# A planner that leaves room for TensorE's instruction transfers, and the order that comes from it

## The chip, the cores and the metric

The kernel runs on one core of a Trainium2 chip. The metric is the device time of one execution in microseconds (us); the kernel before takes 1061.63 us (median of three runs, 1060.88 to 1062.44). The engines are TensorE (PE in the profile; its weight loads are PEld), VectorE (DVE), ScalarE (ACT), GpSimd (POOL) and SyncE (SP), which issues the transfers of the weights.

## The reference

A trunk of two layers over 256 tokens of width 1024, all in float32. Layer 0 mixes the tokens with an RWKV-7 recurrence, layer 1 with stick-breaking attention; 12 heads of 64 do this, and 4 heads attend to 256 fixed memory tokens.

```python
def swiglu(x, w_gate, w_up, w_down):
    return (jax.nn.silu(x @ w_gate) * (x @ w_up)) @ w_down
...
    for i in range(DEPTH):
        x = layer_norm(ALPHA * x + 0.5 * swiglu(x, ffn1_w_gate[i], ffn1_w_up[i], ffn1_w_down[i]),
                       ln_g[i, 0], ln_b[i, 0])
        ...
        heads = jnp.concatenate([mix, memory_attention(mq, mem_k, mem_v)], axis=-1)
        x = layer_norm(ALPHA * x + heads @ w_out[i], ln_g[i, 1], ln_b[i, 1])
        x = layer_norm(ALPHA * x + 0.5 * swiglu(x, ffn2_w_gate[i], ffn2_w_up[i], ffn2_w_down[i]),
                       ln_g[i, 2], ln_b[i, 2])
```

The recurrence of layer 0, for each head with a 64x64 state (w is a decay, kk a normed key, b = kk * a):

```python
    def step(state, inp):
        r_t, w_t, k_t, v_t, kk_t, b_t = inp
        sa = jnp.einsum('bhij,bhj->bhi', state, kk_t)
        state = (state * w_t[:, :, None, :] - sa[..., :, None] * b_t[..., None, :]
                 + v_t[..., :, None] * k_t[..., None, :])
        return state, jnp.einsum('bhij,bhj->bhi', state, r_t)
```

## The kernel before, in words

**Tiles.** The tokens lie in two halves of 128. The hidden width of a feed-forward part, 2816, is worked in 11 blocks of 256 columns. Most weights are split into a high and a low part in a type that TensorE takes in one pass (float32r), and so are the activations; one 128x128 piece of an activation then meets 512 columns of weights in three products (high by high, low by high, high by low; `mm3`). These are the wide split products, printed as `hi_..`, `lo_..` against `xTh`, `xTl` or another `hi_..`. Products left in plain float32 take two passes and count as two (`raw_..` against `hT_945r`, and the gate, `gup_111r`). Transposes go through TensorE too (`cst` against the tile).

**The mixer of layer 0** (`rwkv`) works on chunks of 64 tokens: it builds a triangular inverse T with small products of 64x64 (12 heads by two chunks give 24 or 48 products in one step), then carries the 64x64 states S along. In the profile's names: `Tt_332r,Lm_333r` is Lm times Tt, whose result Y goes through VectorE or ScalarE into `Y_340r,T_339r` and `T_339r,Y_340r` (T by Y, in both orders); this is done twice, the second time with the larger blocks (`lastl`). `vn_314r,Sk_344r` is Sk by V, `S_113r,qr_377r` the state by queries, `L_345r,Tt_332r` is Tt by X, where X lies in a buffer that the trace calls L. In the text, "Lm.Tt", "T.Y", "S.qr" and "L.Tt" stand for these. Between such steps lie copies and sums on VectorE and ScalarE, each step waiting for the one before. The mixer of one half is issued beside blocks of the feed-forward part of the other half (`alternate`), and the wide products of those blocks fill TensorE while the mixer's steps wait.

**The order.** Nothing is issued when the program is written down. Each instruction is first recorded in a `Plan` as an operation; products that belong together (`together`) form one. `price` gives each its duration on its engine. `order` is a list scheduler: it plays the engines forward with a clock for each, transfers that land one behind the other (`LAND`), a TensorE clock that halves after a window of 3413 ns that was too idle (`WINDOW`), and extra time when TensorE changes between kinds of product. At each step it takes the engine that can go on first and, of the operations that could start there, the one of the least rank:

```python
                t, o = x
                p = o.pri + (t - t_e) * WAIT
```

`o.pri` comes from a table of numbers, `URGENCY`, one for each operation, unpacked in `improve`; the table is the result of a search that was done ahead of time. So the order on every engine, and the buffer that every tile gets, follow from the table and from the times that `order` reckons. `issue` then writes all instructions in that order. As it does so from one line, every instruction has the same line in the profile (L767 before, L787 after), and they are told apart by the names of their tiles.

Of the kernel before, what the change touches and what calls it, by code (L numbers as in the profile page):

```python
# [113 lines left out]
class Op:  # L114
    __slots__ = ("i", "eng", "calls", "took", "lag", "after", "opens", "closes", "pri", "func", "port", "left", "ready",
                 "end", "users", "kb", "turns", "mode", "share", "spent", "fine", "parts", "round", "places", "ways")


class Engine_:
# [11 lines left out]
WINDOW = 3413.0  # L131
ROUNDS = 50
# [3 lines left out]
    'c-l?edDu=>)Iad^B%+Y1P)Q;s6=fbmL?lCo43#-UGDb2Kp(0~4&lJi~B2qFWDnq778YLo%l9KT3-)Fz~dtLAEkLS9Fv(MgZeb;w=*V^Zt`>FG32;'  # L136
    'DOz$(YPZa^&9-K1@rJwg3C~|G)2T%nwPDq@4=kY488JDoO72I{vaGS$!#lSw8>i^Wncjc;RFS<DGLbYwGxd%abIhV<&%4ec$EkBzfF-YySMd&yV@'
    'M>W|dtZaGq)i<eE3Hm5^qa7~hY^Gygl%(wHu5PsSjLeq>%@`%4B=5K%b|GnPl-0=rO$bLnVJj$mf{vI&r4Q#x^_+8Q03nBFLdg|^ZnXxZ~D&~FPy'
    'p^&f$$78y&W5n!$|PwEk3xBq<jo@?{Cb=D92?D^`>#)uedpP=J!S8j>`9XGVhH!1PJMpTeE*p1bN=OL)2(cqb8C_m>6#>4#)i-?6KwBHlD*Dpx+R'
    '3~*j(!S5H{YJBp>}6!rb%_?sWb;=6VON$NV*b`-JPv!=9;ZZ^Q0~ehZ-)zw+IXBu)4<%wHz{KE<}K#&luFmDV0mAW1s?9K!C0lVtPc5OTIjl6qf+'  # L140
    'aBN2i#lE)weMvI^E-`*Jgu*qG<X+zuGXJ^GN%CO9B>CIt*R5S;eF%95C&`{gA!IbZ>=HH^b2WRHR!fp~FNKh+gn3ql@b^t{5%2fl*u4}VHiR&ft('
    'Eg6NkOkWDksU)+fw+nHtxdBNm3u)bIak)<`AZx3*ldLjgLGy9KsP;oq$`lTax5qz8vkFB-eEb;T9OoESV(3jk^MdpRwz&A8`;C2R6dmoa<npOi7Z'
    '=14H-)Kd-KuBoE<M^O+(1$*-&458=h8NwT<QlH^(zLT>ym3e!LLgs>e)3KU9`x$@-6{7G_|c(tx0SIk-as}MSe5a$0A!rfvu@}m%Lo5{ZEAzTZ$o'
    'P4O`c*8OL+MFbHCx)=<l_c4=B7_c;tb<2Oe=!zUbK%_ZoJo=oFLsqrk`go0lDqn3LzpvR!M$lohQ8_Hs%@9T)-t#wo@W{)N!E(|U!Nqimxr(%*D~'
    '?tCpdI1oFu<-dBQVEGS=FgaNtMW-Ebm=+u?JHALWaMFyxxFWHOFyY!pISb7sZk_V_dMSO`7X{rR;?GV0MJx#!yu?!t$XzI%m@C1BH<&)<G0M&fwh'
    'Yj!a_$DgCK#T>uxy@zgy*%{oaAO>y4bU&WFg>z5do+KUK;YYO)t{01U#J6}a`68}oa6POJ;SDj(^(LQ=hA_i=@6v#Q@}o7shv3<Pen~QJaR{eimz'
    '7QBehOg<9Z3_%+ed{^>Q#Il7s4~n&CRD~rITb6j0>I#VH;oH!L2dIt*hwxt`H`Rc{8!T*Vrn?mYW2??df4aWBOs8p13g@*Oz&pzLHK_r`^Nwe>O>'
    'OWBWP24DFaC#quS|8=G)!wXrz!!M*gX3S39RuxAL3%y$wFSJJR2`TJmVIVuls64#q?sInNWkedte^Mp98kw3HLb7%3Lz{f(yjg})T*MzX8I2+|;A'
    'G)>|PUT^A$nhg$))^L)AAt$ono3iC=oP}K7m}o<cyAE1dcUWKi7j9_0ap%&&?4#~JmxP?l4;dx9)A8lJcNsLaP$M(*qh!w0SlZu)Lv}GwAm;012<'
    '04$GNm`u(gi1k~g2xM!epQ$64h>L%!6d599ZT&<RIttqmdJ)1?XG^nQ{orziczaFsC)x%ATW>EX5GG~wE`WL+`ZG#*yV!~}=RiqqacNm64se?AZ4'  # L150
    '>sm>2wjT{(=RfQ};QT-5CdoyypIIYG?%tLjJ{^%HBVc))?WbY2KjLiOqcFTvd^YCB54rlNxQ(xuB>fMCkVU@CS{lNbm+--w-^zswa)06|c0T7kTH'
    '0j*orQHDnp_ut?X7WyKHbnTgpTt4NppSx@4xt)9mh)1q!n^v6MkI{`-L!mPo8w67oW1ZHIDS1>ph-df609L=$G+pKS+{!uq%p3-@KS4P0P>`d0eb'
    'T2$#u+XX$oXnzWgAyhroO!*bSxN%Dn!Z{u||-Y*i5^Yn54)({rfrZMk?@GyLa{mo~3To;$l!{tW2d~Bik$cqW=Z6Hqy%l-1Sw>i!GaGso@d%eByL'
    '1(MT-MWwYtD2Uqm9Gook^PP&`Gn@2_)<R0^<i@GBemimzK+GEx9}n(j&xRcK9&oI<m9(FdS!jQeB9jQljIk@z$ZnlCl<}=N>Kj_@aGx2@E-l_N|X'
    'EKQiJHuIC}QH^Y2x24jEGnPH(YmspG@xO&V_QksH6ziVkplN6qLYPw!TDo4}z*rx4zMH%Y$2)0yg2ad_P$M>dJs65RL%r~VV${`}~R3q7qf(K=1&'
    ';SroTKsT0&*=QKuME7smtIk=wzu2Q^vg}BD7+y&X)u1zK%5SiESdQKDI1b=h<t|CG=%e(I^$U5Y4hG!VCH5m8Ns?d1YQBDE6FXY5_lS7>DG#1x<6'
    'wRr!RO`T*OpHF0*AZIcK{|g(}QkwZo1rjMa}(EZr%##wLb3_lRu4{50laKCI|jpaYb5k_2qgA{mH*@=;Qm@;#gL!{^r*xIOSnaS3KGaqc7>-1{$!'
    '3&J3lQQ|bITylV}IQaDwLO_oXWJ6=RDQ;ilz-D-<de~4uk{8=HVM&Q=ZY;WEpEm=55je~1xc6U_=&Y5SgI@5~%jg83-vwZZVAnmwLyyx-dC;TqRm'
    '!`fe37^99un&75^!grdeSy=5aVgFD2WjIxeCoSK??|sZ!){9vJxli_`GcK3V0tzC?lSgT#~$L}rJ{N+e9z0K^7#H8Tjs?YMT={R$yL@G;oQ}Htj&'
    '(s9D9i^*{u7!&*}8=O*yxc4MqI*H1BA!Xvoi(<oavQt<KKt<X>@fG{dP&I9nS}+u?l&>)#3Q+i`ZQc+F+s+idvwJ@JrBIVY!dW)OdGG}lp>|Kjr*'  # L160
    '@0Ze!oce)@#<ir`!`Rfz`fGe&Tg(o@a=IXOG`0iIY&Z8e?0-G>UgjGKhhcIiBmWP|w@;iK_X-7l*U|Z9jj!$f65oFidsVNcW6ZsF!k=aIw5<2L^='
    'YN#el=LNe9AmDq@>svrFWZr&ScC+J<An%eLxIf;d43I{iXfMgDd^zQgdsyHEy1D^Rs`rdiWWeUbkLmyxw5$1MnN*csn*7cW(WdTXdj;oc&XdzOT-'
    'Gq_+NyS0!-iCiC57-okKgBA3>S$xpC-%zAH`uaG%z&@b-x{>#WEuM4b~h2Fnw{l2i(+9svpb<9}HCQ3qh2yP>2^d5P<$+%<mKR+I{laoW(b2(e~>'
    'e)t5#cRD&V_G@NT#s90HQbh(?@AncpM9r%e$MM9I`Ecx=J@_*7>&UH%I1DU9UCO?Uc{~E#PC6L?8D1F&UpeJT^KbGP8}Q{35S1H;w=0sdjDKkdFc'
    '2q^W~L?+s%_pO+A92^JwptY}Lvo>)7`MziNxc0vdDHy!Ea~@o5?S;{NS6cC|BRCEp)lLnG&16pKfld&c`WY1n>xQba!Ig>N=<jNlvSlk>EqTZ0fX'
    'Tf2pR@M$sV!oCj9ogxROm}iRk+)-bA*zZs%BLCh}yLa=s1MF^|M(=6(P&%{A`d!#j7miu^wv3*Y*Dv&BYkPBM6086C`nGtU<HPs`eAC|ze;fYns^'
    'k0}>R&UxO+8%MH3V0?(-`BYsI!N~^`hFlQydr4<L>zUy1F+9e=A#W8lS$h_TO+RV69R2TkC9UpS^)*J*nS&Tpx5u{F+<OvSFWb0spRtNpZc;?d-c'
    '!E|#Z3E!mi`VX}T<5>Ag%-|DL)4XyE#F<bex6HmLrbsj9bz;nNOnwnz+Os5;u!xVqm`#q!9Opn^Zmbc`789BNXKc?c#!|KwGq3ofNv*LIdY`5<&c'
    '0Lu0aq8KRbiReT_wv0yd*j+4>MJg&jY|aPZh8Gt)HX32gCnJ_^Rw6a=AXf~+A-cZ)K1{Du(OCBvY<W$%pvN|Q!v|Wo*MAj3x})3|0bN-;k6(>{-A'
    'E}V$Yk_Z7Y`xi|GOw&Qdqeu{#rvHdSZx+nd)ke+g^d`k@|2-|!Xv9tF#`wL-|C7Ppl<qv3gv{c0w9`vM#mIX(kd%Uh$8n*Fx^YLnWR<!<|sE%Na('  # L170
    'wZ$Hws&(q~`7Pt;i^r4pkk_->6v-+!{>|^!{)W@-g7|l@n5T=!JqE0!LnYPKcJR2(+-upnN8MagfzRwIgd3A+MZ6Y~f$a@pH6EtrG{-BfJ6$d61='
    'E`&7mUq)S;~(?bZNi$Bk*>#`n>9CdrLk4MO^s<&Kqc6R{YDt&d<fHWv-N#?zjFtxW8%6&*Aw6-!C^$7F^yXzp7gQKCy{9f7ZE;_*zk~_Px0L2=@j'
    '0ya%_WB{Pephwk`N_5r;L40^_EDdzZ2{b;Ax9%=8B8+V%1>oIt8mw4vZFEx@^jo5Jv2KVXhuC0=)eJjN9a+nRcM(^wUa-Sth3;p##JxJ}i7sasy)'
    '+h&?@#@D4@qNIY7o2~PPglx`oA@z|?Xd@5jthJB_s{tJ20tpv^9Rh))10+(+rPqgvG*0>aDlIb;M2{R<NUnrJ~11NBXF8YpElB$>=6_8^%H{|5cn'
    'd^JgrZ>L_gQjr|ZP&^0!lc*b{hC$Xp*9-<_5<euI9giBHq&IY&~pWUe0I5A$ZA7e~Y}BMi>S-?jRd1A5Ahifcvweceq@FjS7=(hIOFqX?ZA<9}dy'
    '8itqSWlz3G?d=5TuYI4L)?_sI2kd%EOoT0YOq_GD`AgqD=Dg>{<x@VbqB-N>6R)>LjYfg+l)pxB`2nuq@~3eQ{IOR&Yrhb$kF|>&=1Whn|Czjjn0'
    'zU}dWier+^Igco_&4QPU<8duBV&NTjLSqhw`<7JzyG)%CL88U)YO%zQ~L6VmnB#^5tEh@1#keIqz0Ev=q;pu9Lg=-5u4hoZ`1ZjJ5OOJR7&s=#Ry'
    '$JwGR~p{1HTO+(&-UR*{KPn++4#{z$6#G3E>`}lZWtYa`6h%=qUEHiAr5aX3_-oeggZ25|<#pve<TzlF+v8OS|#;1pTY~KLie~dXOj{RZrlKyL;{'
    'lpabkNE)~%=4$U8tV%)^ZzfLoCoBmt@RFj?lX1_OlIQBM%>$v+vD)DtYejF%4l)wZjEDXU1<K^ZPJoMFQ$iuxE$2^241s^+hSbYhKsr7^p)bVz}O'
    'F?KE_^weebZNgni{w@2mOy!#Pd(O%B8F_BfyXkm~Plj(cPJnXu*AAANrzJ#^D|A6S_lGSig1<$4)fSrF$s^5IAM(aie{-uKbV&Zc!`*i_%%v<wW&'  # L180
    '@^`6v+|S(EaO{++GqC9bEf`lir5m4#%~$3*&8D^Ty}O?9Z}YWq?4sCDD~PLa$OksvMvs>AZKz)A3%RjhZ}gsc{zbd9&9Db|&O&SSH(vqcZ}HkmZC'
# [106 lines left out]
class Plan:  # L288
# [1604 lines left out]
```

## Time and profile before

| what | value |
|---|---|
| median of three runs | 1061.63 us (1060.88 to 1062.44) |
| profiled execution | 1061.31 us, span 1059.5 us |
| mean granted clock of TensorE | 0.994 |
| busy | TensorE 1041.7 us (98%), VectorE 883.6 (83%), ScalarE 740.9 (70%) |
| products | 6275 |
| instruction transfers of TensorE's queue (q8) | 49, 0.80 MB |
| moved by DMA | 303.19 MB, 286 GB/s on average |

The span is the time from the first to the last instruction in the profile; 1.8 us of the execution lie around it. Times in a row of the timeline are the start and the length of an instruction; the ends of products are modelled and overlap, so that the distance of two starts is what a product costs. A bracket at the end of a row is the idle time of the engine ahead of it, and what ended that.

### The profile page before, as it was taken

What the parts mean: (1) busy time and instruction counts of PE and PEld (TensorE: products, weight loads), DVE (VectorE), ACT (ScalarE), POOL (GpSimd) and SP (SyncE); (2) the same over time, 40 slices, a digit from 0 to 9 for tenths busy, and PEclk for the clock granted to TensorE, in tenths of its full rate; (3) what the DMA queues carried; (4) which work ended last, traced back from release to release, by engine and by line L of the source; (5) the groups of instructions that cost most, each with busy time, mean ns of one, the idle gap of its engine ahead of it and who ended that gap; (6) DMA issues with size and microseconds to landing.
All of it is one profiled execution on the core that took longest, in us unless ns stands there. A gap on an engine that the chain in (4) does not pass through costs nothing.

```text
span 1059.5 us, 17849 instructions
## 1 busy us (share of the span) xinstructions
PE 1041.7 (98%) x6275; PEld 835.5 (79%) x6275; DVE 883.6 (83%) x1241; ACT 740.9 (70%) x1065; POOL 5.3 (0%) x20
## 2 busy tenths in 40 slices
PE   9999999999899999999999999999999999999996
PEld 7888888877688776688888888888778777878885
DVE  6676679999899997898799755469899999976688
ACT  6665559968689887667677544457987998865572
POOL 0000000000000000000000000000000000000000
PEclk9999999999899999999999999999999999999998
DMA  9997869779399788799899966677989989997891
GB/s 327 329 369 242 270 215 352 247 253 336 115 338 328 255 264 290 242 339 329 284 340 366 325 211 215 193 255 254 370 297 313 364 285 304 368 349 258 276 311 67
DMA packets 212684, 303.19 MB, mean 286 GB/s; under 512 B 13892, under 2 KB 159728, under 8 KB 212594
## 3 DMA queue, kind: packets, MB, share of 16 engines
q1 hardware_dynamic: 212050, 301.53, 85.5%
q8 instruction: 49, 0.80, 0.3%
q10 hardware_dynamic: 544, 0.52, 0.2%
q14 instruction: 41, 0.34, 0.1%
HBM read 300.95 MB, written 1.05 MB: 285 GB/s over the span
## 4 chain that ended last, share of the span: by engine, by line
PE 97%; DVE 1%; ACT 1%; DMA 0%; issue 0%; SPq 0%; DVEq 0%; ACTq 0%
PE ps_29r L767 30%; PE ps_30r L767 28%; PE ps_27r L767 8%; PE ps_26r L767 8%; PE ps_3r L767 8%; PE ps_25r L767 8%; PE ps_5r L767 4%; PE ps_6r L767 3%; DMA raw_12r<-in_ffn_w_up_dram 0%; DVE x L767 0%; DVE L_345r L767 0%; SPq L767 0%; ACT hi_10r L767 0%; ACT Lm_333r L767 0%; DVE lo_11r L767 0%
## 5 line engine op out<-in xcount | busy, mean ns | idle before, releaser
L767 PE MATMUL ps_29r<-hi_13r,xTh 128*128 128x512 f32 x64 | 26.3, 411 | 0.0
L767 PE MATMUL ps_29r<-hi_43r,xTh 128*128 128x512 f32 x64 | 26.0, 406 | 0.0
L767 PE MATMUL ps_29r<-lo_14r,xTh 128*128 128x512 f32 x66 | 25.8, 390 | 0.0
L767 ACT ACTIVATE idle_2r<-ps_29r 128x256 f32<-128x256 f32 (+1 forms) x31 | 12.8, 411 | 18.4 <-PE ps_29r L767 18.3
L767 PE MATMUL ps_29r<-hi_46r,xTh 128*128 128x512 f32 x62 | 25.1, 405 | 0.0
L767 PE MATMUL ps_29r<-hi_43r,xTl 128*128 128x512 f32 x64 | 25.1, 392 | 0.0
L767 PE MATMUL ps_29r<-hi_13r,xTl 128*128 128x512 f32 x64 | 25.0, 391 | 0.0
L767 PE MATMUL ps_29r<-hi_46r,xTl 128*128 128x512 f32 x62 | 24.2, 390 | 0.0
L767 PE MATMUL ps_29r<-lo_44r,xTh 128*128 128x512 f32 (+1 forms) x62 | 23.8, 383 | 0.0
L767 PE MATMUL ps_30r<-lo_11r,xTh 128*128 128x512 f32 (+1 forms) x62 | 23.8, 383 | 0.0
L767 PE MATMUL ps_29r<-lo_11r,xTh 128*128 128x512 f32 x58 | 22.8, 392 | 0.7 <-DVE lo_11r L767 0.7
L767 PE MATMUL ps_30r<-hi_46r,xTh 128*128 128x512 f32 (+1 forms) x58 | 23.0, 396 | 0.0
L767 PE MATMUL ps_29r<-hi_7r,xTh 128*128 128x512 f32 x54 | 22.6, 419 | 0.1
L767 PE MATMUL ps_30r<-lo_17r,xTh 128*128 128x512 f32 x58 | 22.6, 390 | 0.0
L767 PE MATMUL ps_29r<-lo_8r,xTh 128*128 128x512 f32 x58 | 22.6, 390 | 0.0
L767 PE MATMUL ps_29r<-lo_17r,xTh 128*128 128x512 f32 x58 | 22.6, 390 | 0.0
L767 PE MATMUL ps_30r<-lo_47r,xTh 128*128 128x512 f32 x58 | 22.6, 390 | 0.0
L767 PE MATMUL ps_30r<-hi_46r,xTl 128*128 128x512 f32 (+1 forms) x58 | 22.2, 383 | 0.0
L767 PE MATMUL ps_30r<-hi_22r,xTh 128*128 128x512 f32 x54 | 22.1, 410 | 0.0
L767 PE MATMUL ps_29r<-hi_16r,xTh 128*128 128x512 f32 x54 | 22.1, 409 | 0.0
L767 PE MATMUL ps_30r<-hi_10r,xTh 128*128 128x512 f32 x54 | 22.1, 409 | 0.0
L767 PE MATMUL ps_29r<-lo_47r,xTh 128*128 128x512 f32 x56 | 21.8, 390 | 0.0
(2125 smaller groups left out, 3922.4 us busy)
## 6 DMA issues: line engine op xcount, KB each, us to landing
raw_21r<-in_ffn_w_down_dram SPq DMA_DIRECT2D x19, 512.0 KB, 5.4
raw_67r<-in_ffn_w_gate_dram SPq DMA_DIRECT2D x32, 256.0 KB, 5.8
raw_67r<-in_ffn_w_up_dram SPq DMA_DIRECT2D x32, 256.0 KB, 6.0
raw_15r<-in_ffn_w_down_dram SPq DMA_DIRECT2D x16, 512.0 KB, 6.0
raw_12r<-in_ffn_w_gate_dram SPq DMA_DIRECT2D x31, 256.0 KB, 4.0
raw_12r<-in_ffn_w_up_dram SPq DMA_DIRECT2D x31, 256.0 KB, 4.6
raw_45r<-in_ffn_w_gate_dram SPq DMA_DIRECT2D x31, 256.0 KB, 6.3
raw_45r<-in_ffn_w_up_dram SPq DMA_DIRECT2D x31, 256.0 KB, 5.5
```

The lines of the kernel that those rows point to most:

```text
L767: fn(*[at(x) for x in a], **{n: at(x) for n, x in k.items()})
```

## The change

The planner gets a model of how TensorE's own instructions arrive. Each operation counts the products that it issues (`count`: one for a transpose or a float32r product, two for a plain float32 one). In `order`, the count of products issued so far runs over edges, at 94.7 and then every 127.1 products. Two edges may not be passed within less than 5500 ns: where they would be, the operation in which the second one lies takes as much longer. Nothing is issued for this; it only changes the clock by which the scheduler chooses. The table of urgencies is another one (298 lines), found with the new clock.

```diff
+FETCH = 5500.0
+CHUNK = 127.1
+CHUNK0 = 94.7
...
 URGENCY = (
-    'c-l?edDu=>)Iad^B%+Y1P)Q;s6=fbmL?lCo43#-UGDb2Kp(0~4&lJi~B2qFWDnq778YLo%l9KT3-)Fz~dtLAEkLS9Fv(MgZeb;w=*V^Zt`>FG32;'
...
+    'c-l?e2iVT#8$R&+Ata(i%E-u!5DjESnUx|+8dhdzLRRskkeN}*%9gC8XegsnW-3L6QWTX{M0xK2=iB=~j{m>ocn|M0zW06I*L9xfbzaZ&eQWe_j6'
...
             o.i, o.eng, o.calls, o.after, o.parts, o.ways = len(self.ops), eng, [], {}, [], {} if either else None
+            o.count = 0
...
             o.mode, o.round = (rows <= 64, m <= 64), st.dtype == F32R
+            o.count += 1 if method == "transpose" or st.dtype == F32R else 2
...
         mode, until, busy, cold = None, WINDOW, 0.0, True
+        issued, edge, crossed = 0, CHUNK0, -FETCH
...
                     until, busy = until + WINDOW, share * rest
+                first, took_, stall = issued, took, 0.0
+                issued += o.count
+                while issued > edge:
+                    at_ = t + stall + took_ * (edge - first) / o.count
+                    if at_ < crossed + FETCH:
+                        stall += crossed + FETCH - at_
+                        at_ = crossed + FETCH
+                    crossed = at_
+                    edge += CHUNK
+                took = took_ + stall
             clock[e] = t + took
```

The operations stay the same; their order, and the buffers, change. TensorE has 6275 products before and after. VectorE gets three instructions more and ScalarE three fewer (copies that may go to either), SyncE issues 873 in both.

On TensorE, in the mixer of layer 0 for the first half, these rows stood between the last T.Y products and the last Lm.Tt products of the inverse (banks are named `ps_..`, x2 is two products in one row):

```order
L767 MATMUL ps_25r<-T_339r,Y_340r 64x64 x2
L767 MATMUL ps_5r<-T_339r,Y_340r 64x64 x2
L767 MATMUL ps_25r<-T_339r,Y_340r 64x64 x2
L767 MATMUL ps_5r<-T_339r,Y_340r 64x64 x2
L767 MATMUL ps_26r<-Tt_332r,Lm_333r 64x64 x2
L767 MATMUL ps_6r<-Tt_332r,Lm_333r 64x64 x2
```

The same place in the new order:

```order
L787 MATMUL ps_26r<-T_339r,Y_340r 64x64 x2
L787 MATMUL ps_5r<-T_339r,Y_340r 64x64 x2
L787 MATMUL ps_30r<-hi_40r,hi_46r 128x512
L787 MATMUL ps_30r<-lo_50r,hi_46r 128x512
L787 MATMUL ps_30r<-hi_40r,lo_47r 128x512
L787 MATMUL ps_30r<-hi_40r,hi_46r 128x512
L787 MATMUL ps_30r<-lo_50r,hi_46r 128x512
L787 MATMUL ps_30r<-hi_40r,lo_47r 128x512
L787 MATMUL ps_25r<-Tt_332r,Lm_333r 64x64 x2
L787 MATMUL ps_6r<-Tt_332r,Lm_333r 64x64 x2
```

Six wide split products of a feed-forward block now stand between the two groups of small ones; the edge after 1493 products lies in the Lm.Tt block in both.

On TensorE, in the mixer of layer 0 for the second half, ahead of the first L.Tt products, before:

```order
L767 MATMUL ps_3r<-vn_314r,Sk_344r 64x64 x2
L767 MATMUL ps_27r<-vn_314r,Sk_344r 64x64 x2
L767 MATMUL ps_3r<-vn_314r,Sk_344r 64x64 x2
L767 MATMUL ps_27r<-vn_314r,Sk_344r 64x64 x2
L767 MATMUL ps_26r<-raw_48r,hT_945r 128x512
L767 MATMUL ps_6r<-L_345r,Tt_332r 64x64
L767 MATMUL ps_5r<-L_345r,Tt_332r 64x64
```

and now:

```order
L787 MATMUL ps_6r<-S_113r,qr_377r 64x64 x2
L787 MATMUL ps_5r<-S_113r,qr_377r 64x64 x2
L787 MATMUL ps_26r<-raw_67r,hT_945r 128x512
L787 MATMUL ps_30r<-hi_7r,xTh 128x512
L787 MATMUL ps_30r<-lo_47r,xTh 128x512
L787 MATMUL ps_30r<-hi_7r,xTl 128x512
L787 MATMUL ps_30r<-hi_7r,xTh 128x512
L787 MATMUL ps_30r<-lo_47r,xTh 128x512
L787 MATMUL ps_30r<-hi_7r,xTl 128x512
L787 MATMUL ps_5r<-L_345r,Tt_332r 64x64
L787 MATMUL ps_6r<-L_345r,Tt_332r 64x64
```

The block of Sk.V products that stood here now comes behind the L.Tt products, and six wide split products stand between S.qr and L.Tt; the edge after 3145 products lies in the L.Tt block in both.

More of the change, by code (lines that the diff above doesn't have):

```diff
@@ L115 @@
     __slots__ = ("i", "eng", "calls", "took", "lag", "after", "opens", "closes", "pri", "func", "port", "left", "ready",
-                 "end", "users", "kb", "turns", "mode", "share", "spent", "fine", "parts", "round", "places", "ways")
+                 "end", "users", "kb", "turns", "mode", "share", "spent", "fine", "parts", "round", "places", "ways", "count")
 class Engine_:
@@ L141 @@
[L141 to L145, printed above, removed]
```

291 lines of the change are left out of this document (150 added, 141 removed).

## The prediction

> **What bounds the kernel now.** I read the page first: the busy times, the slices and the chain that ended last.
>
> ```profile
> span 1059.5 us, 17849 instructions
> PE 1041.7 (98%) x6275; PEld 835.5 (79%) x6275; DVE 883.6 (83%) x1241; ACT 740.9 (70%) x1065; POOL 5.3 (0%) x20
> PE   9999999999899999999999999999999999999996
> PEclk9999999999899999999999999999999999999998
> q8 instruction: 49, 0.80, 0.3%
> PE 97%; DVE 1%; ACT 1%; DMA 0%; issue 0%; SPq 0%; DVEq 0%; ACTq 0%
> ```
>
> TensorE is busy for 1041.7 of 1059.5 us, and its clock is whole but at the ends and in the slice around 275 us. The edit keeps all 6275 products, so nothing can be won but the 17.8 us in which TensorE idles, the slow stretch, and what products lose where one kind follows another. The queue that brings TensorE's instructions made 49 transfers of 0.80 MB, which is 16 KB each and 6275 / 49 = 128 products each. Second, the waits of TensorE, which say what the idle time waits for (us in total, times, longest):
>
> ```profile
> PE ps_6r L767 <- issue: 2.0, 2, 1.4
> PE ps_6r L767 <- DVE L_345r L767: 1.7, 1, 1.7
> PE ps_5r L767 <- ACT Lm_333r L767: 0.7, 1, 0.7
> PE ps_5r L767 <- DVE S_113r L767: 0.7, 1, 0.7
> ```
>
> The top row has no releaser in the data: "issue" is idle time in which nothing that the profile shows was waited for. The timeline (start, length) has its two places. Windows of TensorE alone (length, busy time, products, granted clock, share of the DMA engines, GB/s) say, from the start on, how many products came before, and, for the two stretches that end in a stall, what the DMA engines did meanwhile:
>
> ```profile
> 258.06 0.21 PE L767 MATMUL ps_6r<-Tt_332r,Lm_333r 64*64 64x64 f32 x1 [0.67 <-issue]
> 418.38 0.21 PE L767 MATMUL ps_6r<-L_345r,Tt_332r 64*64 64x64 f32 x1 [1.36 <-issue]
> 0.00:252.31 252.31, 249.68 (x1366) 1.00 0.88 292
> 0.00:258.05 258.05, 254.76 (x1494) 1.00 0.89 294
> 0.00:263.41 263.41, 260.11 (x1619) 1.00 0.88 294
> 0.00:269.88 269.88, 266.03 (x1748) 1.00 0.89 295
> 0.00:401.21 401.21, 394.25 (x2763) 0.99 0.85 283
> 0.00:405.91 405.91, 398.95 (x2891) 0.99 0.85 282
> 0.00:411.63 411.63, 404.67 (x3018) 0.99 0.85 283
> 0.00:418.37 418.37, 410.01 (x3148) 0.99 0.85 284
> 252.31:258.05 5.74, 5.08 (x144) 1.00 1.04 381
> 411.63:418.37 6.74, 5.33 (x143) 1.00 0.97 311
> ```
>
> The stalls come at products 1494 and 3148. They are 1654 apart, 13 x 127.2, and 94.7 + 127.1k (the change's own numbers) gives 1493 at k = 11 and 3145 at k = 24. So I take both for waits on the transfer that brings the next 128 products, asked for when the edge before was passed: it was there 5.74 and 6.74 us after that, with the DMA engines full of weights (shares 1.04 and 0.97). Products of 64x64 make an edge come early. Edges 4.70 us (401.21 to 405.91), 5.36 us (258.05 to 263.41) and 6.47 us (263.41 to 269.88) after the last one had no such stall, so the transfer's time varies between below 4.7 and 6.74 us.
>
> **What the change does, part by part.** The extra slot and the loop cost nothing on the chip: they only set the order. What it moves I price by these rows.
>
> ```profile
> 413.73 0.27 PE L767 MATMUL ps_6r<-S_113r,qr_377r 64*64 64x64 f32 x2
> 414.48 0.22 PE L767 MATMUL ps_3r<-vn_314r,Sk_344r 64*64 64x64 f32 x1
> 259.61 0.38 PE L767 MATMUL ps_5r<-cst,idle_2r 128*128 128x128 f32 x2
> 259.75 0.48 PE L767 MATMUL ps_29r<-hi_16r,hi_7r 128*128 128x512 f32 x1
> 260.06 0.39 PE L767 MATMUL ps_29r<-lo_14r,hi_7r 128*128 128x512 f32 x1
> 260.29 0.40 PE L767 MATMUL ps_29r<-hi_16r,lo_47r 128*128 128x512 f32 x1
> 409.35 0.91 PE L767 MATMUL ps_27r<-gup_111r,zl_315r 128*128 128x384 f32 x2
> 410.10 1.02 PE L767 MATMUL ps_25r<-raw_48r,hT_945r 128*128 128x512 f32 x2
> ```
>
> A block of 48 small products takes 414.48 - 413.73 = 0.75 us, 0.016 each. A wide split product (128x512) takes 0.23 (260.06 to 260.29), the first one after transposes 0.31 (259.75 to 260.06), 0.08 more. A gate pair (128x384) takes 0.75. I counted the products between edges in both orders.
>
> *Edge 11* (k = 11, layer 0, first half). Between edges 10 and 11 stood 118 small products and 9 wide ones; now 115 and 12. Without its stall the stretch took 5.74 - 0.67 = 5.07 us at most. The six wide products now ahead of the last Lm.Tt block and the three taken out earlier are net +3 x 0.23 = 0.69, and a wide run between small blocks costs about another 0.1: 5.8 us, where the transfer needed 5.74. Nothing is left of 0.67, with almost no margin.
>
> *Edge 24* (second half). The stretch had 121 small products, 3 wide, 2 of the gate and 2 plain ones; now 116, 6, 4 and 2. 6.74 - 1.36 = 5.38 us, and 0.69 + 0.75 - 5 x 0.016 more: 6.7 us against 6.74. Nothing is left of 1.36, again without margin.
>
> *Edge 13.* Here the stretch loses three wide products (115 small, 6 wide, 4 gate before; 118, 3, 4 now): 6.47 - 0.69 + 0.05 = 5.8 us. If the transfer comes as at edge 11 that is no stall, if as at edge 24 it is 6.74 - 5.8 = 0.9. I take the middle, 0.5. Edge 22 goes the other way (4.70 us and six wide products more, two plain ones less) and had no stall. Edges 12, 23 and 25 change by three wide products or fewer. All others have 128 products of about 0.23 us, 29 us, and no stall.
>
> So the stalls give 0.67 + 1.36 - 0.5 = 1.5 us, bounds 0 (transfers come later by what was put in) and 2.0. Time put in front of an edge is not lost: those products have to be done anyway, and only move from elsewhere.
>
> The Trainium skill, "Runtime: NRT & Kernel Launch", section "Instruction fetch mechanics", says that instructions come in 16 KiB blocks fetched while the current ones execute, and that a crossing costs a queue's tail bump, "mostly hidden". The trace agrees at 46 or so of 48 edges and in the 16 KB; at two it has 0.67 and 1.36 us. By that sentence alone the stalls would be worth nothing, and the sum would lack its 1.5 us.
>
> *Transposes.* In the new order 125 wide products come first after a group of transposes, 132 before: 7 x 0.08 = 0.6 us, bounds 0 and 1.0 (other neighbours of different kinds, up to 4 x 0.1).
>
> *Data waits and the slow stretch.* The tail of layer 0's mixer (S.qr, L.Tt, kn/bn, memory attention; products 1785 to 2012) is in the same order as before. There lie the waits for L_345r (1.72), Lm_333r (0.73) and S_113r (0.65), and the half clock:
>
> ```profile
> 274.20 0.27 PE L767 MATMUL ps_6r<-L_345r,Tt_332r 64*64 64x64 f32 x1 [1.72 <-DVE L_345r L767]
> 425.88 0.27 PE L767 MATMUL ps_5r<-L_345r,Tt_332r 64*64 64x64 f32 x1 [0.58 <-DVE L_345r L767]
> 271.37:274.78 3.41, 1.69 (x72) 1.00 0.31 118
> 274.78:281.61 6.83, 5.45 (x117) 0.50 0.17 41
> ```
>
> TensorE was busy for 1.69 of 3.41 us, and the next 6.83 us ran at 0.50 of the clock. The wait of 1.72 began at 272.48, so it ends 0.58 ahead of the window's end and begins 1.11 behind its start: arriving 0.7 to 0.8 us earlier leaves it inside. So I take 0 for the waits and for the slow stretch; below nothing up to -2.7 (half of 5.45, all of the slow stretch), above it up to +4.4 (the last rival). The 0.58 at 425.88 has six wide products of cover before and after: 0. VectorE's and ScalarE's work is the same but for three copies that change engine, and lies beside TensorE's; SP's 873 instructions are as many, in other buffers. Start and last LayerNorm: the same chains, 0.
>
> *Sum:* -1.5 - 0.6 = -2.1. The profiled execution took 1061.31 (1059.5 of span and 1.8 around it), which makes 1059.2; the runs' median, 1061.63, is 0.3 above it: 1059.5. As the edges that lose their stall have no margin I leave 0.1 of stall there: **1059.6 us**.
>
> **The rivals.** *The slow stretch goes too.* At 418 us 1.36 us idle, which leaves at least 0.60 of a window of 3.41 us busy, did not cost the clock; 0.50 busy did. If L_345r comes 0.4 us earlier for TensorE, or the wait slips over the window's edge by as much, the clock stays. Worth up to 2.7; the two waits inside the stretch (0.73, 0.65) are for VectorE and ScalarE and would take up to 1.4 back; the middle is 2.0: 1057.6. For it: only 0.1 of the clock's share decides. Against: the order there is untouched.
>
> *The gain is given back.* The chain of VectorE and ScalarE between the mixer's steps, not the stall, sets the pace, or the transfer takes 6.7 us at each close edge and stalls at 13 for what 11 won, while edge 24 is passed later but no less late. Then only the transposes' 0.6 remain: 1061.0. For it: full DMA engines in both stretches, no margin at either edge. Against: the waits' rows name no other engine there. The skill's rule ("mostly hidden") would leave the same time, since the two stalls would then have another cause that the order need not touch; the edges' spacing speaks against that.
>
> *Slower.* The six wide products (1.4 us and 0.3 for the changes of kind) now stand ahead of the last Lm.Tt block of layer 0's first half. What VectorE makes of that block comes 1.7 us later, less the 0.67 of the stall that goes: 1.0. If the chain from there to L_345r has no slack, the wait at 272.48 grows from 1.72 to 2.7 us, since the filler that covered it has been used up. With over 0.7 more idle the wait passes the window's end at 274.78 (it ended 0.58 ahead), the next window is thin too, and the half clock lasts two windows longer: 1.0 + 6.83 / 2 = +4.4, 1064.0. It decides from a wait 0.6 longer on. For it: TensorE runs into that wait already. Against: between the two places lie some 290 products with about as many wide ones as before, which move with the block.
>
> **How the numbers follow.** About 0.2%, 2.1 us, is what a measurement of this kernel can tell from no change: faster means below 1059.5, slower above 1063.75. The forecast has 0.47 (its own range 1058.6 to 1060.9, which the bound cuts: 0.22 faster, 0.25 same), the slow stretch gone 0.17 (faster), the gain given back 0.16 (same), the same by the skill's rule 0.03 (same), slower 0.17. So faster 0.39, same 0.44, slower 0.17. The range leaves out the slower case: low 1059.6 - 2.7 = 1056.9, high 1061.6 with nothing won and 0.9 of a new stall at edge 13, 1062.5.
>
> **What would show it.** In the profile after: the same 6275 products and 49 transfers; the waits' "issue" row without 0.67 and 1.36, and if any, at edge 13, about product 1747; Lm_333r, S_113r and L_345r waits of the same size and a half clock of two windows at about 274 us. "Issue" waits that add up to 1.5 or more at other edges say that the gain was given back; an L_345r wait over 2.3 with a third window at 0.50 is the slower case; a whole clock there is the faster one. I am wrong as to the cause if stalls end at products that are no multiple of 127 apart, or go while the time stays.

## The result, and the profile after

The changed kernel takes 1057.94 us (median of 12 executions, 1057.12 to 1060.08), the kernel before 1060.62 us (12 executions) on the same chip. The ratio is 0.9974, with a 95% interval of 0.9965 to 0.9983: 2.8 us faster. A second comparison, of 10 executions, gave 0.9981 (0.9970 to 0.9991). The profiled execution took 1057.22 us, with a span of 1055.4.

The page's busy line and slices, and the waits of TensorE, of the kernel after:

```profile
span 1055.4 us, 17854 instructions
PE 1039.9 (99%) x6275; PEld 833.1 (79%) x6275; DVE 885.6 (84%) x1244; ACT 737.7 (70%) x1062; POOL 5.4 (1%) x20
PEclk9999999999999999999999999999999999999998
q8 instruction: 49, 0.80, 0.3%
```

```profile
PE ps_6r L787 <- DVE L_345r L787: 1.8, 2, 1.2
PE ps_5r L787 <- ACT Lm_333r L787: 0.9, 1, 0.9
PE ps_5r L787 <- DVE S_113r L787: 0.6, 1, 0.6
```

Products and instruction transfers are as many as before. No row of the waits has "issue" any more: both stalls are gone, and none has come at edge 13 or elsewhere. The wait for L_345r is down from 1.72 to 1.21 us, and the slow slice around 275 us has its whole clock. The stretches between the close edges, as windows of TensorE alone (edges 10 to 11, 11 to 12, 12 to 13; 22 to 23, 23 to 24, 24 to 25):

```profile
252.27:258.13 5.86, 5.86 (x141) 1.00 1.05 390
258.13:264.06 5.93, 5.93 (x132) 1.00 0.84 290
264.06:269.94 5.88, 5.35 (x143) 1.00 1.03 375
402.91:409.15 6.24, 6.24 (x130) 1.00 0.74 248
409.42:415.70 6.28, 6.28 (x143) 1.00 1.00 364
415.70:422.60 6.90, 6.34 (x140) 1.00 0.83 273
```

All six last over 5.8 us. Before, the ones ahead of the two stalls lasted 4.83 and 5.1 us and then waited. The stretch ahead of these six, from edge 21 to 22 (397.91 to 403.15), lasts 5.24 us and ended without a wait, too.

Where the time went between the two profiled executions follows from the starts of the products. At the counts below, the same products (by kind) lie behind TensorE in both, so that the differences are costs and not moved work.

| products | before, us | after, us | difference | what lies there |
|---|---|---|---|---|
| 0 to 1174 | 219.07 | 219.31 | +0.24 | |
| 1174 to 1487 | 36.99 | 37.73 | +0.74 | six wide products alone between small ones; about half of it |
| 1487 to 1588 | 4.27 | 3.32 | -0.95 | the first stall |
| 1588 to 1790 | 10.35 | 10.39 | +0.04 | |
| 1790 to 1992 | 13.77 | 11.81 | -1.96 | half clock before, whole after |
| 1992 to 3029 | 126.75 | 126.90 | +0.15 | |
| 3029 to 3159 | 7.37 | 5.61 | -1.76 | the second stall |
| 3159 to 5142 | 397.47 | 397.28 | -0.19 | |
| 5142 to 5363 | 37.53 | 36.88 | -0.66 | other executions of the order of before: -0.4 to -0.5 |
| 5363 to the end of the products | 195.83 | 196.08 | +0.26 | |

### The profile page after: what moved, and what is told of

Same layout as the page of the kernel before. It is cut to its first block, busy times and chain, and to the rows that moved or that the text cites. A ratio compares the mean times of both kernels' runs of the same rounds, so it can differ in the third digit from the quotient of the medians.

```text
span 1055.4 us, 17854 instructions
## 1 busy us (share of the span) xinstructions
PE 1039.9 (99%) x6275; PEld 833.1 (79%) x6275; DVE 885.6 (84%) x1244; ACT 737.7 (70%) x1062; POOL 5.4 (1%) x20
## 4 chain that ended last, share of the span: by engine, by line
PE 97%; DVE 1%; DMA 1%; ACT 0%; issue 0%; SPq 0%; DVEq 0%; ACTq 0%
PE ps_29r L787 29%; PE ps_30r L787 28%; PE ps_27r L787 8%; PE ps_26r L787 8%; PE ps_25r L787 8%; PE ps_3r L787 8%; PE ps_5r L787 4%; PE ps_6r L787 3%; DMA raw_12r<-in_ffn_w_up_dram 1%; DVE x L787 0%; DVE L_345r L787 0%; SPq L787 0%; DVE st_573r L787 0%; DVE lo_11r L787 0%; ACT hi_10r L787 0%
## 5 line engine op out<-in xcount | busy, mean ns | idle before, releaser
L787 PE MATMUL ps_29r<-lo_11r,xTh 128*128 128x512 f32 (+1 forms) x70 | 27.0, 385 | 0.8 <-DVE lo_11r L787 0.8
L787 PE MATMUL ps_29r<-hi_46r,xTh 128*128 128x512 f32 (+1 forms) x68 | 27.1, 398 | 0.0
L787 PE MATMUL ps_29r<-hi_46r,xTl 128*128 128x512 f32 (+1 forms) x68 | 26.2, 385 | 0.0
L787 PE MATMUL ps_30r<-hi_16r,xTh 128*128 128x512 f32 (+1 forms) x64 | 25.4, 397 | 0.0
L787 PE MATMUL ps_30r<-hi_16r,xTl 128*128 128x512 f32 (+1 forms) x64 | 24.6, 385 | 0.0
L787 PE MATMUL ps_30r<-lo_14r,xTh 128*128 128x512 f32 x62 | 24.2, 390 | 0.0
L787 PE MATMUL ps_30r<-lo_11r,xTh 128*128 128x512 f32 x62 | 24.2, 390 | 0.0
L787 PE MATMUL ps_29r<-lo_41r,xTh 128*128 128x512 f32 x60 | 23.4, 390 | 0.0
L787 PE MATMUL ps_30r<-hi_46r,xTh 128*128 128x512 f32 x58 | 23.4, 403 | 0.0
L787 PE MATMUL ps_30r<-hi_43r,xTh 128*128 128x512 f32 x56 | 22.8, 407 | 0.0
```

The source lines that it names most:

```text
L787: fn(*[at(x) for x in a], **{n: at(x) for n, x in k.items()})
```

## The experiments

### Do the stalls follow the count of products?

Tiny products among the warm-up move every edge to an earlier place in the work and leave the order alone. The edit stands in `issue` in both kernels (`shift` starts at 24 in the order of before and at 32 in the changed one):

```diff
+        shift = 24
...
                 for fn, a, k in o.calls:
                     fn(*[at(x) for x in a], **{n: at(x) for n, x in k.items()})
+                if o.eng == "PE" and shift:
+                    fn, a, k = o.calls[0]
+                    for _ in range(shift // 2):
+                        fn(*[at(x[:32, :32]) for x in a], **k)
+                    shift = 0
```

Expected of `before_shift24`:

> The order of before with 24 tiny products among the first warm-up products: each edge falls 24 products earlier in the work. Theory A: the two issue waits move to products 1469 and 3121 of the work and grow, since the stretches ahead of them are 4.6 and 3.7 us: about 1.1 and 2.5 us; a third of up to 0.6 may come at edge 14. Time 1 to 2.5 us over before. Rival C: the waits stay at products 1493 and 3145 of the work with 0.67 and 1.36 us, or their size does not change; time 0 to 0.8 us over before.

Measured: 1065.96 us, ratio to before 1.0034 (1.0019 to 1.0049). The two larger rows of the timeline with "issue", and windows from the start to them:

```profile
258.59 0.33 PE L768 MATMUL ps_25r<-T_339r,Y_340r 64*64 64x64 f32 x4 [0.64 <-issue]
419.00 0.26 PE L768 MATMUL ps_3r<-vn_314r,Sk_344r 64*64 64x64 f32 x1 [3.24 <-issue]
0.00:258.58 258.58, 256.21 (x1495) 1.00 0.88 293
0.00:418.99 418.99, 409.24 (x3148) 0.99 0.85 283
```

The stalls are now in other steps (T.Y and Sk.V instead of Lm.Tt and L.Tt), but at the same counts, 1495 and 3148, where before had 1494 and 3148. The second grew from 1.36 to 3.24 us, as its stretch got shorter; the first did not grow. A third, of 0.34 us, came at edge 23, where none was forecast. The time rose by 3.6 us, more than either theory had: 1.1 us of the profile's difference are the tiny products themselves, which delay the start, and a half clock follows the second stall.

Expected of `after_shift32`:

> The changed kernel's order with 32 tiny products (32x32, results never read) among the first warm-up products, so that each edge falls 32 products earlier in the work. At the start they cost up to 1 us, partly hidden by the wait for x; read off at the first edge. Theory A: the stretches that end at products 1461 and 3241 of the work are only 4.0 and 4.6 us long, so issue waits of 1 to 2.7 us at the first and 0.5 to 2 us at the second come back; time 2 to 4 us over the changed kernel. Rival C (the order is faster for its neighbours of kinds and its data waits, the edges have nothing to do with it): no issue wait, at most 1 us over the changed kernel.

Measured: 1063.22 us, 1.0016 (1.0004 to 1.0028) of before, where the changed kernel has 0.9974. The stalls are back, and the two larger ones are these:

```profile
258.48 0.27 PE L788 MATMUL ps_5r<-T_339r,Y_340r 64*64 64x64 f32 x2 [1.59 <-issue]
425.77 0.21 PE L788 MATMUL ps_5r<-S_113r,qr_377r 64*64 64x64 f32 x1 [1.17 <-issue]
0.00:258.47 258.47, 255.13 (x1494) 1.00 0.88 293
0.00:425.76 425.76, 417.79 (x3275) 1.00 0.85 282
```

They lie at edges 11 and 25 (94.7 + 127.1k gives 1493 and 3272); a third, of 0.26 us, lies at edge 14. The time is about 4.5 us over the changed kernel, where theory A had 2 to 4; 1.3 us of it are the tiny products at the start. Without these it would be about level with before, so the changed order is no faster by itself: it is faster where its edges fall.

### What holds the transfers up?

In the order of before, five transfers of weights of 512 KB, issued between 246 and 258 us, bring only a quarter of their rows (`before_cut`); `before_cut_both` does the same, too, to seven transfers issued between 404 and 413 us. No instruction moves. The edit shown is that of `before_cut`; the other adds the last seven transfers of 256 KB or more ahead of the second half's first L.Tt products.

```diff
...
+        at_ = order.index(LMTT[0, True])
+        loads = [o for o in order[:at_] if o.kb >= 512][-4:] + [o for o in order[at_:] if o.kb >= 512][:1]
+        for o in loads:
+            o.calls = [(fn, tuple(x[:32] for x in a), k) for fn, a, k in o.calls]
```

Expected of `before_cut`:

> The order of before; five transfers of 512 KB (pieces of the output and the next projection's weights, issued between 246 and 258 us) bring only a quarter of their rows, so the values that use them are not the reference's. Theory D (TensorE's instruction transfer waits behind the weights in the DMA engines): with a share of the DMA engines of about a half instead of 1.04 between edges 10 and 11, the transfer comes before the 4.8 us of that stretch are over and the issue wait of 0.67 us at product 1494 is gone or under 0.2; the wait of 1.36 us at 3148 stays. Rival E (the transfer takes 5.7 us whatever the DMA engines do): both waits stay.

Measured: 0.9993 (0.9984 to 1.0001) of before. The stretch from edge 10 to 11, and the one row with "issue":

```profile
252.72:257.53 4.81, 4.81 (x142) 1.00 0.73 175
417.23 0.21 PE L773 MATMUL ps_6r<-L_345r,Tt_332r 64*64 64x64 f32 x1 [1.64 <-issue]
```

With the DMA engines' share at 0.73 where it was 1.04, the first stall is gone, although the stretch lasts 4.81 us as ever. The second is still there, as forecast, and the interval of the time holds 1: the first stall alone is worth too little to be seen in it.

Expected of `before_cut_both`:

> The order of before with the cut of before_cut and, issued between 404 and 413 us, seven more transfers (output and gate and up weights, ln_b) that bring only a quarter of their rows; values that use them are not the reference's. Theory A with D (both issue waits are transfers of instructions held up behind weights, and they are most of what the changed kernel wins): both issue waits are gone or under 0.3 us with every product where it was; the mean granted clock over the runs goes up too if the second wait has cost clock (0.9955 or more, against 0.9944 to 0.9951 of before); time 1.5 to 3 us under before, as the changed kernel. Rival N (the changed kernel wins by its new order of products, the waits are only part): the issue waits go, but the time is less than 1.3 us under before.

Measured: 1057.61 us against 1061.01, ratio 0.9969 (0.9959 to 0.9979). The two stretches that end in the stalls, and the only "issue" row left:

```profile
252.36:257.18 4.82, 4.82 (x140) 1.00 0.91 168
410.48:415.45 4.97, 4.97 (x141) 1.00 0.17 47
257.64 0.21 PE L773 MATMUL ps_6r<-Tt_332r,Lm_333r 64*64 64x64 f32 x1 [0.24 <-issue]
```

The order of before with (nearly) no stall is as fast as the changed kernel: 3.3 us (2.2 to 4.4) are won without moving a product. The products stand in the same order in both traces, so the difference can be placed: 0.43 and 1.57 us are won at the two stalls, 0.75 at the half clock of 275 us, which comes and goes (below), and 0.49 between products 5142 and 5363, where all other executions, too, are faster than this one of before. Elsewhere no stretch of the table above differs by over 0.2. At the stalls this is 2.0 us, as much as the changed kernel wins there (-0.95 - 1.76 + 0.74 in the table).

The trace of each run also has the transfers themselves: 49 packets of 16 KB in queue 8, most of them 0.9 to 1.3 us long, one for each edge. The table has nine stretches, in us from the start; five of them end in a stall. The second column is when TensorE passed the first edge, the last when it went on at the second:

| run, edges | edge passed | packet starts | packet landed | TensorE goes on |
|---|---|---|---|---|
| before, 10 to 11 | 252.34 | 255.59 | 256.70 | 258.06, stalled |
| before, 23 to 24 | 411.63 | 416.01 | 416.95 | 418.38, stalled |
| before_shift24, 23 to 24 | 411.41 | 416.69 | 417.66 | 419.00, stalled |
| after_shift32, 10 to 11 | 252.66 | 256.04 | 257.09 | 258.48, stalled |
| after_shift32, 24 to 25 | 419.75 | 423.23 | 424.33 | 425.77, stalled |
| before_cut, 10 to 11 | 252.76 | 254.98 | 256.25 | 257.58 |
| before_cut_both, 23 to 24 | 410.47 | 412.24 | 413.16 | 415.40 |
| changed kernel, 10 to 11 | 252.28 | 255.65 | 256.76 | 258.14 |
| changed kernel, 23 to 24 | 409.43 | 412.32 | 413.26 | 415.69 |

In each stall TensorE goes on 1.34 to 1.44 us after the packet has landed, whether it stalled for 0.67 or 3.24 us; where the packet landed at least 1.33 us ahead of the edge there is no stall. The packet itself moves in about 1 us. What varies is how long it stands before it starts: 3.25 and 4.38 us after the edge in before, 2.22 and 1.77 with fewer weights on the way. So theory A and theory D hold: the stalls are waits for transfers of instructions that are held up behind weights, and most of what the change wins is won there.

The second cut alone is worth 0.9993 - 0.9969 = 0.24%, 2.5 us (from two comparisons, on two chips), for a wait of 1.36 to 1.64 us. The rest fits the higher clock (below), but was not measured apart from it.

### Which part of the change does it?

`model_alone` is the changed program with the table of before (the edit is shown against the changed kernel):

```diff
 URGENCY = (
-    'c-l?e2iVT#8$R&+Ata(i%E-u!5DjESnUx|+8dhdzLRRskkeN}*%9gC8XegsnW-3L6QWTX{M0xK2=iB=~j{m>ocn|M0zW06I*L9xfbzaZ&eQWe_j6'
...
+    'c-l?edDu=>)Iad^B%+Y1P)Q;s6=fbmL?lCo43#-UGDb2Kp(0~4&lJi~B2qFWDnq778YLo%l9KT3-)Fz~dtLAEkLS9Fv(MgZeb;w=*V^Zt`>FG32;'
...
```

`table_alone` keeps the new table and takes the model's effect away:

```diff
-FETCH = 5500.0
+FETCH = 0.0
```

Expected of `model_alone`:

> The new loop (FETCH, CHUNK, count) with the table of urgencies of before. The order on TensorE differs in 36 rows only; between edges 10 and 11 stand the same 118 small and 9 wide products, between 23 and 24 120 small, 6 wide and 2 plain ones. Theory A (the stalls are waits for TensorE's instruction transfers, and the new table's order took them away): both stretches stay short, about 4.8 and 5.0 us without a stall, so issue waits of about 0.6 and 1.3 us stay at products 1494 and 3147; time within 0.8 us of before. Rival B (the model in the scheduler is what wins): the issue waits are gone and the time is 2 to 3 us under before.

Measured: 1.0011 (0.9994 to 1.0027). The only stall is the first:

```profile
258.12 0.21 PE L783 MATMUL ps_6r<-Tt_332r,Lm_333r 64*64 64x64 f32 x1 [0.67 <-issue]
455.15 0.50 PE L783 MATMUL ps_25r<-hi_10r,hT_1042r 128*128 128x512 f32 x1 [0.47 <-ACT hT_1042r L783]
```

Each theory missed one half: the second stall did go, with 36 rows moved, and the time did not. From edge 23 to 25 this order took 12.7 us where before took 14.4, but from 25 to 27 46.7 where before took 44.7. Of these 2.0 us, 0.9 are waits (0.41 for L_345r, which before has ahead of edge 25, and 0.47 for hT_1042r, the row above); I did not trace the rest.

Expected of `table_alone`:

> The new table with FETCH = 0, so that the loop never adds a stall. The order up to edge 13 and from edge 26 on is as in the changed kernel; around edge 24 the first L.Tt products come in two groups of 12. Stretches 11 and 24 hold 115 small and 12 wide, and 116 small, 6 wide, 4 gate and 2 plain products, as in the changed kernel. Theory A: no issue waits, time within 0.8 us of the changed kernel, 2 to 3 us under before. Rival B (the gain needs the model): an issue wait of 0.5 to 1.5 us at edge 24 or 25, time 1 us or less under before.

Measured: 1.0014 (1.0003 to 1.0025), against 0.9974 with the model. Theory A was wrong here, and so was B's stall: there is no "issue" row. New waits for data stand after edge 25, in the mixer's tail and the next feed-forward part:

```profile
439.78 0.44 PE L787 MATMUL ps_6r<-cst,Y_340r 128*128 128x128 f32 x2 [0.68 <-DVE Y_340r L787]
441.59 0.50 PE L787 MATMUL ps_27r<-hi_49r,xTh 128*128 128x512 f32 x1 [0.69 <-ACT xTh L787]
456.49 0.50 PE L787 MATMUL ps_25r<-hi_49r,hT_1042r 128*128 128x512 f32 x1 [0.47 <-ACT hT_1042r L787]
```

The two stretches from edge 25 to 27 take 48.6 us here and 44.7 in the changed kernel; 1.84 of these 3.9 us are the waits in the rows. My reading, which no run tests, is that the table's numbers are fitted to one reckoning of time; with another, the scheduler takes different products around edge 24 and has them no more when the mixer's tail needs cover. What is shown is that model and table win together, and neither does alone.

In both runs a stall went and the time did not fall, which is close to what the prediction named as a sign that its cause is wrong (stalls that go while the time stays). It does not speak against the cause here, since time was lost at another place, between edges 25 and 27; before_cut_both, where no product moves, shows what the stalls alone are worth.

### Is it enough to put six products ahead of the block?

`before_edge11` takes the order of before and issues the next two operations of three wide products, which stood right behind it, ahead of the last Lm.Tt block. The edit is in `issue`; its last line does the move:

```diff
...
+        order = order[:at_] + moved + [o for o in order[at_:] if o not in moved]
```

Expected of `before_edge11`:

> The order of before with six wide products that stood within the last Lm.Tt block's next rows put ahead of that block, as at this place in the changed kernel, and nothing brought from elsewhere. Theory A (each stretch of 127 products has to last as long as the transfer asked for at its start): the issue wait at product 1494 is gone, since the stretch ahead of it now lasts 6.3 us, but the next one falls from 5.4 to 3.8 us without waits, so an issue wait of 1 to 2 us comes at edge 12 (product 1620); time 0.3 to 1.3 us over before. Rival L (it is the place of the six products that counts): no issue wait near 1494 or 1620, time 0.5 to 0.9 us under before.

Measured: 0.9998 (0.9986 to 1.0009). The stall at 1494 went; the stretch to edge 11 took 6.45 us and the next one 5.05, where before had 4.83 and 6.25. (The second stall, which the edit does not touch, stayed, with 1.09 us.) Instead came this wait:

```profile
260.74 0.33 PE L782 MATMUL ps_6r<-vn_314r,Sk_344r 64*64 64x64 f32 x4 [0.63 <-ACT Y_340r L782]
```

The time lies between the two theories, and the interval reaches both. Rival L had it right that no stall would be left at 1494 or 1620, and wrong that this alone would win time. Theory A's wait at edge 12 did not come: the stretch lasted 5.05 us and not 3.8. What took the stall's place was a wait for the mixer's chain (Y, made from the block that now comes later), the kind of cost that the prediction's slower case had named.

### Where does the clock come in?

The profiled executions of before and after differ by 1.96 us in the half clock at 275 us, but one pair proves little: the same program run again (`after_again`, no edit) had it there, in the second of these two windows:

```profile
273.45:276.86 3.41, 1.48 (x42) 1.00 0.04 14
276.86:280.27 3.41, 3.09 (x80) 0.50 0.02 5
```

So I went by the mean granted clock, which each execution lists. It is an indirect measure: the half clock of the last 3.6 to 7.0 us, which every profiled execution shows, is in it, too. Four edits bear on it; the first two only exchange two neighbouring sums on VectorE, which stood in different order in the two kernels:

```diff
...
+        pair = EVEN_ODD[0, 1]
+        i, j = sorted(order.index(o) for o in pair)
+        order[i], order[j] = pair if 0 == 0 else pair[::-1]
```

(In `after_unswap` the last line has `1 == 0`, and takes the reversed pair.) `after_again` is the changed kernel with no edit.

Expected of `before_swap`:

> The order of before with one edit on VectorE: the two neighbouring sums into X of the first half's second chunk (even and odd heads) change places, so that the even heads come first, as in the changed kernel. Theory S (this swap, not TensorE's order, shortened the wait for L_345r from 1.72 to 1.21 us and with it made the half clock behind it rarer): the wait is 1.2 us, the mean granted clock over the runs rises from 0.9944 by about 0.001, the two issue waits of 0.67 and 1.36 stay, time 0.7 to 1.7 us under before. Rival T (the wait got shorter because TensorE's products moved): the wait stays 1.7 us, time within 0.5 us of before.

Expected of `after_unswap`:

> The changed kernel with the same two sums put back in the order of before (odd heads first), nothing else. Theory S: the wait for L_345r is 1.7 us again, no issue waits, the mean granted clock over the runs falls by about 0.001, time 0.7 to 1.7 us over the changed kernel. Rival T: the wait stays near 1.2 us, time within 0.5 us of the changed kernel.

Expected of `after_again`:

> The changed kernel once more, beside the others on the same chip. All theories: 2 to 3.5 us under before; no issue waits; a mean granted clock over the runs of 0.996 to 0.997 against 0.994 to 0.995 of before. Whether the half clock after the L_345r wait of 1.2 us appears in the profiled execution depends on where the windows of 3.41 us fall: with or without.

The other two put an idle product into the wait:

```diff
+        o, cst = FILL[-1]
+        fn, a, _ = o.calls[0]
+        o.calls = [(fn, (a[0].tensor[:], cst[:, :P], cst[:, :512]), dict(start=True, stop=True))] + o.calls
```

Expected of `before_fill`:

> The order of before with one idle plain product of 128x512 (two passes, 0.86 us, its result overwritten) ahead of the L.Tt products of the first half's second chunk, in the wait for L_345r. Theory H (the half clock comes from idle time within one window of 3.41 us, and this wait of 1.72 us is the most of it): the wait falls to about 0.8 us, the half clock after it becomes rare, the mean granted clock over the runs rises from 0.9944 to 0.995 to 0.9965, time 0.5 to 1.8 us under before; the issue waits stay. Rival G (the half clock has another cause): clock and time as before within 0.4 us.

Expected of `after_fill`:

> The changed kernel with the same idle product in its wait of 1.21 us. Theory H: the wait falls to 0.3 us; the half clock there, which came in one of three profiled executions of this order, goes; mean clock up by 0 to 0.0008 and time 0 to 0.8 us under the changed kernel (2 to 3.5 us under before), which would make it the fastest of all. Rival G: as the changed kernel within 0.3 us.

| kernel | executions | mean clock | ratio to before (95%) |
|---|---|---|---|
| before (in four comparisons) | 109 | 0.9948 | 1 |
| before_swap | 12 | 0.9954 | 0.9993 (0.9983 to 1.0004) |
| before_fill | 12 | 0.9957 | 1.0003 (0.9995 to 1.0012) |
| before_edge11 | 11 | 0.9946 | 0.9998 (0.9986 to 1.0009) |
| before_shift24 (second stall longer) | 8 | 0.9929 | 1.0034 (1.0019 to 1.0049) |
| after_shift32 (stalls at edges 11 and 25) | 12 | 0.9946 | 1.0016 (1.0004 to 1.0028) |
| before_cut (first stall gone) | 11 | 0.9950 | 0.9993 (0.9984 to 1.0001) |
| model_alone (second stall gone) | 12 | 0.9954 | 1.0011 (0.9994 to 1.0027) |
| table_alone (both stalls gone) | 12 | 0.9953 | 1.0014 (1.0003 to 1.0025) |
| before_cut_both (both nearly gone) | 12 | 0.9962 | 0.9969 (0.9959 to 0.9979) |
| changed kernel, and again | 12 + 10 | 0.9964 | 0.9974, 0.9981 |
| after_unswap | 11 | 0.9967 | 0.9981 (0.9970 to 0.9992) |
| after_fill | 9 | 0.9970 | 0.9973 (0.9964 to 0.9982) |

The executions of before had 0.9944 beside the two shifted kernels, model_alone and table_alone, and 0.9948 to 0.9951 beside the others, so a mean is best read against its own comparison.

The exchange did not carry it: the wait for L_345r came out at 1.5 us in both, in before_swap from 1.72 and in after_unswap from 1.21, and after_unswap is as fast as the changed kernel beside it. Theory S fell, and what shortened this wait is only half known. (after_again came as expected, but for one "issue" wait of 0.23 us at edge 11: the margin there is as thin as I had it.) The idle product had to wait itself, 1.24 us on before, for the sum into L_345r on VectorE, and so gave back in delay what it may have won in clock; it neither confirms nor refutes theory H, and after_fill is no faster than the changed kernel.

With the order of before the clock is higher without the second stall (0.9962 against 0.9950 with the first gone alone), and in model_alone and table_alone, which lack it, it is 0.001 above their own executions of before. Of the six profiled executions that have this stall, with 0.99 us or more, two show the half clock behind it. Windows of 3.41 us of before_swap, with the second stall in the first, and of before_shift24, the one with the stall and the three after it:

```profile
418.70:422.11 3.41, 1.77 (x16) 1.00 0.91 284
422.11:425.52 3.41, 3.41 (x54) 0.50 0.62 184
414.63:418.04 3.41, 1.13 (x74) 1.00 0.87 306
418.04:428.28 10.24, 9.28 (x89) 0.50 0.48 159
```

After 1.77 us busy of 3.41 the clock halved; after 2.05 (the changed kernel at 270.90) it did not:

```profile
270.90:274.31 3.41, 2.05 (x60) 1.00 0.22 88
274.31:277.72 3.41, 2.52 (x86) 1.00 0.02 5
```

These two give no sharp limit. Counted in the windows of all the profiled executions, up to the last LayerNorm, the clock halved behind each of the seven with 1.08 to 1.48 us busy and fell from whole behind none with 2.05 or more. Between them it went either way: before_edge11 kept the whole clock behind a window with 1.69 us busy (271.25 to 274.66) and after_unswap behind one with 1.92 (272.21 to 275.62), while before_cut lost it behind 1.94 (273.11 to 276.53).

## Why the prediction was right, and where its steps were off

**What bounds it, and the cause of the stalls: right, and shown.** They follow the count of products, not the work, they end at a fixed time after the packet of instructions has landed, and they vanish when fewer weights are on the way. The change's rule asks for 5.5 us between edges, by the scheduler's own clock. On the chip the two stretches that stalled last 5.86 and 6.28 us where they lasted 4.83 and 5.1, and one, from edge 21 to 22, comes out at 5.24. No stall is left where I allowed 0.5 for edge 13 (its stretch came out at 5.88, where I had 5.8).

One step of this was off: in the sums for each edge I took 5.74 and 6.74 us for what the transfer needs at each place, as if that were fixed. At edge 24 the stretch came out at 6.28, 0.5 short of 6.74, and there was still no stall, because the packet, too, landed earlier: 3.83 us after edge 23, where before had 5.32. At edge 11 it landed as late as before (4.48 and 4.36 us after edge 10), and there the longer stretch did it. The Trainium skill, "Runtime: NRT & Kernel Launch", section "Instruction fetch mechanics", calls the crossing "mostly hidden". That holds wherever 127 products last long enough; here two edges had 0.67 and 1.36 us, and 3.24 when moved.

**The stalls' term, -1.5: the size was off in two parts that nearly cancel.** The starts of the products show -0.95 and -1.76, more than the idle time of 0.67 and 1.36, since products run out ahead of a stall and start up behind it. Against it stands +0.74 ahead of edge 11: I priced a separate run of wide products between small blocks at 0.1, and the run of six cost 0.3 to 0.4. The other half lies ahead of edge 10, and I did not trace it. These rows are the last T.Y row ahead of it, its first and last product, and the first Lm.Tt row (six products are 6 x 0.23 = 1.38, and the distance from first to last row, in which the four small products of the first row lie too, is 1.81):

```profile
256.21 0.28 PE L787 MATMUL ps_5r<-T_339r,Y_340r 64*64 64x64 f32 x4
256.43 0.50 PE L787 MATMUL ps_30r<-hi_40r,hi_46r 128*128 128x512 f32 x1
257.69 0.40 PE L787 MATMUL ps_30r<-hi_40r,lo_47r 128*128 128x512 f32 x1
258.02 0.27 PE L787 MATMUL ps_25r<-Tt_332r,Lm_333r 64*64 64x64 f32 x2
```

Net, the two places gave -2.0.

**Transposes, -0.6: not seen.** Outside the stalls and the half clock the ledger's rows add up to +0.24 + 0.04 + 0.15 - 0.19 - 0.66 + 0.26 = -0.16, and most of the -0.66 is in before_cut_both, too (-0.49 with the order of before), so most of it is no effect of the order. Counting one change of kind (132 to 125) and not the others was the mistake.

**The slow stretch, 0: wrong as a mean, and the rival that had it go was right in part.** In the profiled pair the slow stretch went, as the rival had it, but after_again had it, so this pair shows no effect of the order. I looked for the clock at the wait for L_345r alone. The mean clock rose by 0.0016 from before to after; executions of before at 0.994 took 1061.6 us on average (43 of them), at 0.995 1060.4 (28), at 0.997 1059.7 (12), so 0.0016 goes with 1 to 2 us. The runs put at least part of that on the second stall: without it the order of before has 0.9962. How much of the rest is the shorter wait for L_345r stays open. At the place of the second stall I had seen 1.36 us idle and a whole clock in one execution and taken it as safe; whether the stall lies in one window or in two varies from one execution to the next.

**The rivals.** The gain was not given back in the changed kernel, but it was in model_alone, table_alone and before_edge11, in part to waits for data; the rival's doubt was sound. The slower case did not come: the wait for L_345r fell from 1.72 to 1.21 us where it was to grow to 2.7.

**The sum.** -2.1 was forecast, and -2.8 (-3.7 to -1.8) and -2.0 (-3.2 to -1.0) were measured: stalls more, clock more, transposes nothing. That the sum came this close is in part luck, since the clock, which I had at 0, took the place of the transposes. In absolute time 1059.6 was forecast and 1057.94 measured; 1.0 of this difference is the kernel before, with 1060.62 us beside the changed one where its first three executions had a median of 1061.63.

## What to carry to other kernels

When idle time has no releaser, count the instructions that came before it: on this kernel stalls that came a multiple of 127.1 products apart were transfers of instructions. A shift of the count by a few dummy instructions shows it in one run, and so does the landing of the instruction queue's packets beside the end of each stall. A stretch of products too small to last as long as such a transfer can be stretched by wide ones from a neighbouring stretch: here that gave 2.0 to 2.8 us, with a table fitted to it. Fewer weights on the way at that time gave 3.3, in a run that left three quarters of some weights out; whether the same transfers moved to another time would do as well is not shown. A new cost in a planner changes every later choice, so it has to be fitted again with its table (neither alone won here), and one profiled execution says little on a half clock that depends on where windows fall.

## What the runs showed of the hardware

- TensorE waits for its instructions after 94.7 products and a multiple of 127.1 more if the stretch before is shorter than the transfer takes: 5.74 and 6.74 us with the DMA engines' share at 1.04 and 0.97. In the second of these, 4.38 us passed before the packet of 16 KB started, 0.94 us while it moved, and 1.43 until TensorE went on. With the share at 0.73 a stretch of 4.81 us had no stall, and with 0.17 one of 4.97. The share alone does not decide: with 0.87, before had none in the 4.74 us from edge 21 to 22, where the packet started 1.29 us after the edge.
- A stall in TensorE's instructions can also cost clock: a window of 3.41 us with 1.77 us busy was followed by one at half clock, one with 1.13 by three. The Trainium skill, "TensorE: Matmul & The Clock Gate", Part 1, has the clock fall after an idle window; here windows with up to 1.48 us busy were enough each time, and some with up to 1.94.
- The same program, executed again, has the half clock in some executions and not in others: the changed kernel ran with mean clocks from 0.995 to 0.998.
